# A Transformer block on one Trainium2 core: the order of gates, outputs, norms and index work in the retention stage

## The chip, the cores and the metric

The kernel runs on one core of a Trainium2 chip. A core has a matrix engine (TensorE, PE in the profile; PEld is its weight load), three engines for elementwise work (VectorE or DVE, ScalarE or ACT, GpSimd or POOL), and SyncE (SP), which here only issues DMAs. Each engine works through its own queue in order and waits on semaphores for the others. The time is the device time of one execution in microseconds (us), lower is better; three executions of the kernel before give 1562.02, 1562.23 and 1563.64, a median of 1562.23.

## The reference

One hybrid block over 512 tokens of width 1024 and 16 meta tokens ahead of them (528 in all): a gated feed-forward layer, a mixer, a second gated feed-forward layer, with norms between. The mixer projects the normed input `u` with one wide matrix and feeds two branches:

```python
proj = u @ w_in   # rq, rk, rv, rg, aq, ak, av, iq, ik, iw, g_ret, g_att
yr = retention(rope(rq), rope(rk) * 256**-0.5, rv)     # 4 heads, keys 256, values 512 wide
yr = (silu(rg) * yr) @ w_ret_out                       # yr is normed per head first
ya = dsa_attention(rope(aq), rope(ak), av, rope(iq), rope(ik), iw, 128) @ w_att_out
merged = sigmoid(g_ret) * yr + sigmoid(g_att) * ya
```

Retention is a product of queries and keys, weighted by a decay matrix per head, times the values, and each head's result is divided by its root mean square over its 512 values. Attention has 8 heads of 128. For each query an index score is worked out first: `sum over 8 index heads of iw * relu(iq . ik)`; the 128 best keys by that score (and the meta tokens) are the only ones that the attention of that query sees.

## The kernel before

All products are taken in three parts: both operands are split into an upper and a lower half (`hi`, `lo`), and `mm3` (line 145) issues hi x hi, lo x hi and hi x lo. So each weight tile needs an upper half on ACT (line 284), a lower half on DVE (line 285) and then 24 matmuls, 8 depth blocks of three.

The kernel goes in stages: the first feed-forward layer, projections of values and index and of head 0's queries and keys, the retention stage (about 555 to 924 us), attention (924 to 1116 us), the output projections, the second feed-forward layer. The change lies in the retention stage and the first 20 us of attention.

The retention stage is a list of steps, one for each weight tile, that `steps_through` (line 289) runs: at step i it issues the DMA of tile i+4, the upper half of tile i+2, then the step's matmuls, then the lower half of tile i+2, and then whatever stands "behind" the step. Work may also be put between the depth blocks of a step (`between`: at block k, do this). The order on PE, ACT and DVE is the order in which the program is written (`tc.manual_schedule`); SP and POOL are planned. PSUM has a small pool of four banks (`sm_tile`) for tiles of 512 columns and a second pool of two (`mm_tile`).

Per head h of the four:

- `gates_of(h)` (line 1536): four steps that make psrg; `silu` puts each through ACT into an `sg` buffer, of which there are two. Behind them for h > 0: `values_in(h)`, which splits the values into `vo` hi and lo, and `weigh(h, c)` for c = 0, 1, 2.
- `decayed(h)` (line 1421): the products of keys and queries (psst, 30 matmuls in five tiles), each multiplied on DVE by the decay table `u` (line 1439) and split.
- `weigh(h, c)` (line 1460): 13 matmuls into pspv, multiplied on DVE by the gate (line 1467) into a `to` tile, squares added to `ossum` on ACT and DVE.
- `norm_start(h)` and the generator `rstd_steps`: column sums of `ossum` by four small matmuls (line 218), power on POOL (line 227), a diagonal on DVE (line 232), split, and a product with ones that spreads the result over all rows (psn, line 242), copied to `rn`.
- `normed_parts(h)`: four products `to` times `rn` (line 1487), each split into `vo` hi and lo again, in the place of the values.
- `outputs(h)` (line 1634): four steps of 2 x 12 matmuls into psro, which read those `vo` parts; the result is added to the accumulators `accr`. In the first step, SP fetches the next head's values and decay table; behind the last stands `decayed(h+1)`.
- `queries_keys(h)` (line 1590): four steps for the next head's queries and keys, rotated on DVE in pieces (`rope_pieces`).

The order is: gates of head 0; then for h = 1 to 3: queries_keys(h), outputs(h-1), gates_of(h); then two gate tiles (psgate), the first key and query tile of attention (psak, psaq), outputs(3), one more gate tile. Head h-1's last `weigh` and its norm stand behind the steps of queries_keys(h), `normed_parts(h-1)` behind the last of them, right ahead of outputs(h-1).

The index scores are made beside this. `bring_index` (line 1338), at the first gate of head 0, has the inputs brought: `ixs` (index queries, two copies), the tables `cos` and `sin`, the decay table `u`, head 0's values (`vraw`, four DMAs), and the index keys. `index_queries(0..3)` rotate and split the queries (three DVE operations of 1536 columns, one split). `index_steps` (line 1238) makes the scores in twelve "pairs": six matmuls into two pssc tiles, two relus on ACT, two multiply-and-adds on DVE (line 1257). Before, all pairs lie in queries_keys(1), three in each of its four steps. `select_steps` (line 1262) then draws 48 "picks" on DVE: find the 8 largest of a row (line 1269), mark them (line 1270); 16 each for score tiles of 512, 384 and 256 columns. After each 16, one operation makes a bias tile. Picks stand one to three at a time behind later steps; attention needs the bias tiles in turn.

After the steps, attention's first key and query are rotated by `rope_swap` (line 1225): two half copies on ACT, a product with cos on DVE, one with sin on POOL, a sum on DVE. Then come two gate tiles and the first scores (psS).

## Time and profile before

The profiled execution took 1563.07 us, 0.84 above the median of the three; its span is 1561.3 us at a mean granted TensorE clock of 0.99.

| what | before |
|---|---|
| median of three executions | 1562.23 us |
| profiled execution, span | 1563.07, 1561.3 us |
| PE busy | 1527.3 us, 98% |
| DVE busy | 1092.4 us, 70% |
| ACT busy | 728.7 us, 47% |
| POOL busy | 105.7 us, 7% |
| the stretch 555.5 to 936.3: PE, DVE, ACT busy | 357.34, 263.24, 136.81 of 380.8 us |

How to read it: a line such as `L1435 MATMUL psst<-rqk` is line 1435 of the kernel before, engine operation, the tile written and the tiles read. Matmuls are pipelined: a matmul of 512 columns shows 0.39 us, and the next one begins 0.23 us after it. A wait row names who waited for what and for how long. In a row of a stretch of time the numbers after the length are busy times per engine, then the granted clock (1.00 is full speed), then the share of the DMA engines in use and GB/s. "idle before" in a group of instructions is the time that the engine stood still ahead of them, with the last thing that it waited for.

### The profile page before, as it was taken

The numbers are of one execution on the slowest core, as the hardware profiler recorded it, in microseconds if no ns is written. First come the engines' busy times: TensorE is split into PE (matmuls) and PEld (weight loads), VectorE is DVE, ScalarE is ACT, GpSimd is POOL, SyncE is SP. The second block draws the span as 40 slices with busy tenths as digits, with TensorE's granted clock in tenths as the row PEclk, the third lists the DMA queues.
The fourth block names the chain that finished last, engine by engine and source line by source line (L and its number), as shares of the span: only waits on it lengthen the run. The fifth ranks groups of instructions, "written<-read, shape, count | busy, mean of one in ns | idle before, by whom it ended". The sixth has DMA issues, their size and how long they took to land.

```text
span 1561.3 us, 23921 instructions
## 1 busy us (share of the span) xinstructions
PE 1527.3 (98%) x9779; PEld 1374.8 (88%) x9779; DVE 1092.4 (70%) x1670; ACT 728.7 (47%) x1138; POOL 105.7 (7%) x135
## 2 busy tenths in 40 slices
PE   9999999999999979899999999999999999999997
PEld 8999999999888867687888878999888889899996
DVE  4997585776877756667777687666455788576685
ACT  6655362554354434333323337666435446254453
POOL 1000000002110020000000031111002000000000
PEclk9999999999999989899999999999999999999999
DMA  4233233237364271222322233233443223323232
GB/s 164 70 121 101 90 102 115 82 122 237 129 223 148 82 221 42 101 99 76 118 69 82 96 106 100 75 97 89 137 154 114 81 81 109 108 83 135 82 112 91
DMA packets 150701, 173.48 MB, mean 111 GB/s; under 512 B 4928, under 2 KB 122200, under 8 KB 149952
## 3 DMA queue, kind: packets, MB, share of 16 engines
q1 hardware_dynamic: 141952, 151.58, 29.9%
q0 software_dynamic: 3808, 11.38, 2.0%
q10 hardware_dynamic: 4832, 9.00, 1.7%
q8 instruction: 76, 1.25, 0.3%
q14 instruction: 33, 0.27, 0.1%
HBM read 155.94 MB, written 16.01 MB: 110 GB/s over the span
## 4 chain that ended last, share of the span: by engine, by line
PE 85%; issue 7%; DVE 4%; ACT 2%; DMA 1%; POOL 1%; POOLq 0%; ACTq 0%; DVEq 0%
PE psqX L157 13%; PE psd L157 8%; PE psd L2035 7%; PE psqY L157 7%; PE psro L157 4%; PE psvX L1120 4%; PE psrg L157 4%; PE psqZ L157 3%; PE psu L157 3%; PE psga L157 3%; PE psmo L157 3%; PE psat L157 3%; PE psak L157 3%; PE psaq L157 2%; PE psg L157 2%
## 5 line engine op out<-in xcount | busy, mean ns | idle before, releaser
L285 DVE TENSOR_TENSOR wlo<-raw,whi 128x1024 fp32r<-128x1024 f32 (+2 forms) x184 | 197.4, 1076 | 65.7 <-ACT whi L284 65.6
L284 ACT ACTIVATE whi<-raw 128x1024 fp32r<-128x1024 f32 (+2 forms) x184 | 170.0, 925 | 135.3 <-PE psd L157 41.2
L157 PE MATMUL psqX<-tl,whi 128*128 128x264 f32 (+1 forms) x432 | 122.3, 283 | 0.0
L157 PE MATMUL psqX<-th,wlo 128*128 128x264 f32 (+1 forms) x432 | 122.2, 283 | 0.0
L157 PE MATMUL psqX<-th,whi 128*128 128x264 f32 (+1 forms) x432 | 122.2, 283 | 0.0
L118 DVE TENSOR_TENSOR wlo<-raw,whi 128x1024 fp32r<-128x1024 f32 (+1 forms) x60 | 72.3, 1205 | 56.7 <-ACT whi L117 55.7
L284 ACT ACTIVATE whi<-wsum 128x1024 fp32r<-128x1024 f32 x72 | 76.4, 1061 | 70.7 <-PE psd L2035 22.0
L117 ACT ACTIVATE whi<-raw 128x1024 fp32r<-128x1024 f32 (+1 forms) x60 | 62.6, 1045 | 93.9 <-PE psat L157 26.6
L285 DVE TENSOR_TENSOR wlo<-wsum,whi 128x1024 fp32r<-128x1024 f32 x72 | 87.9, 1222 | 12.5 <-ACT whi L284 12.5
L157 PE MATMUL psro<-vo,whi 128*128 128x512 f32 x256 | 86.0, 415 | 10.2 <-ACT vo L284 9.5
L157 PEld LDWEIGHTS psqX<-th,whi 128*128 128x128 f32 x432 | 82.1, 190 | 0.0
L157 PEld LDWEIGHTS psqX<-tl,whi 128*128 128x128 f32 x432 | 82.0, 190 | 0.0
L157 PEld LDWEIGHTS psqX<-th,wlo 128*128 128x128 f32 x432 | 82.0, 190 | 0.0
L157 PEld LDWEIGHTS psro<-vo,whi 128*128 128x128 f32 x256 | 50.6, 198 | 25.6 <-ACT vo L284 10.2
L157 PE MATMUL psd<-hl,whi 128*128 128x264 f32 x352 | 71.2, 284 | 0.0
L157 PE MATMUL psd<-hh,wlo 128*128 128x264 f32 x352 | 70.9, 283 | 0.0
L157 PE MATMUL psd<-hh,whi 128*128 128x264 f32 x352 | 70.6, 282 | 0.0
L2035 PE MATMUL psd<-whi,hh 128*128 128x512 f32 x176 | 68.5, 389 | 0.0
L2035 PE MATMUL psd<-wlo,hh 128*128 128x512 f32 x176 | 68.5, 389 | 0.0
L2035 PE MATMUL psd<-whi,hl 128*128 128x512 f32 x176 | 68.5, 389 | 0.0
L157 PEld LDWEIGHTS psd<-hh,wlo 128*128 128x128 f32 x352 | 54.4, 188 | 0.0
L157 PEld LDWEIGHTS psd<-hh,whi 128*128 128x128 f32 x352 | 54.3, 188 | 0.0
(440 smaller groups left out, 4529.8 us busy)
## 6 DMA issues: line engine op xcount, KB each, us to landing
raw<-in_ffn_w_up_dram SPq DMA_DIRECT2D x22, 1024.0 KB, 5.0
raw<-in_ffn_w_gate_dram SPq DMA_DIRECT2D x21, 1024.0 KB, 5.0
raw<-in_w_in_dram SPq DMA_DIRECT2D x19, 1024.0 KB, 4.9
raw<-in_w_in_dram SPq DMA_DIRECT2D x31, 512.0 KB, 3.5
raw<-in_ffn_w_down_dram SPq DMA_DIRECT2D x24, 512.0 KB, 3.4
w<-in_w_in_dram SPq DMA_DIRECT2D x24, 512.0 KB, 6.8
raw<-in_ffn_w_down_dram SPq DMA_DIRECT2D x12, 768.0 KB, 4.3
raw<-in_w_ret_out_dram SPq DMA_DIRECT2D x8, 1024.0 KB, 4.7
```

The lines of the kernel that those rows point to most:

```text
L117: nc.scalar.activation(hi, src, AF.Copy)
L118: eng.tensor_tensor(lo, src, hi.bitcast(F32), ALU.subtract)
L157: nc.tensor.matmul(o, a[:, k, :], b[:, sl], start=first and k == 0 and i == 0, stop=last and k == nk - 1 and i == 2, skip_group_check=onto)
L284: nc.scalar.activation(hi, src, AF.Copy)
L285: return lambda: nc.vector.tensor_tensor(lo, src, hi.bitcast(F32), ALU.subtract)
L1120: nc.tensor.matmul(d[bank_][t], a, b[:, k, :], start=not onto and j + k + m == 0, stop=j + k == 3 and m == 2, skip_group_check=onto)
L2035: nc.tensor.matmul(ps, a[:, bs], m[:, j, :], start=first and i == 0, stop=last and i == 2)
```

## The change

- Each head's gates stand ahead of the outputs of the head before: the order is queries_keys(h), gates_of(h), outputs(h-1); of the last head only three gates do, the fourth stands behind. For this there are four `sg` buffers.
- `weigh(p, 0..3)` of head p = h-1 stand one behind each step of queries_keys(h). `values_in(h+1)` moves behind outputs(h).
- The norm is cut in pieces: sums at block 6 inside the first gate, the diagonal behind it, the spreading product at block 4 inside the second gate, and the normed parts two and two behind the second and the third.
- `bring_index`: `u` and the four `vraw` DMAs go first on SP. `decayed(0)` stands ahead of all index queries, and the index keys and the rest of the index queries follow later.
- The pairs: two in the last step of queries_keys(1), then 2, 2, 3 and 3 in the four gates of head 1.
- The picks are drawn at other places and fewer beside each step; those left follow behind the last steps.
- At the start of attention the fifth and sixth gate tile and the first rotation stand in program order too, and the rotation's product with sin goes to DVE.

The diff, cut; where the removed lines are long they are left out, since the kernel before shows them.

```diff
--- before.py
+++ after.py
...
@@ -1231,7 +1229,7 @@
             nc.scalar.activation(bv[hi], ps[lo], AF.Copy)
             nc.scalar.activation(bv[lo], ps[hi], AF.Copy)
         nc.vector.tensor_tensor(av, ps, cos, ALU.mult)
-        nc.gpsimd.tensor_tensor(b[:, :n], b[:, :n], sin, ALU.mult)
+        eng.tensor_tensor(b[:, :n], b[:, :n], sin, ALU.mult)
         nc.vector.tensor_tensor(a[:, :n], a[:, :n], b[:, :n], ALU.add)
         return a[:, :n]
@@ -1336,16 +1334,16 @@
         heads = [dict(t=[], sg=[], o=[]) for _ in range(RH)]
         def bring_index():
+            new_decay(0)
+            heads[0]["raw"] = [rt.tile([P, S], F32, tag="to", name="vraw", bufs=4) for _ in range(4)]
+            for c in range(4):
+                nc.sync.dma_start(heads[0]["raw"][c], vst[0, :, c].rearrange("p b d -> p (b d)"))
             nc.sync.dma_start(ia[:, :, :NL], fq[:, :, :NL])
             for r in range(4):
                 o = r ^ 1
                 nc.gpsimd.dma_start(ib[32 * r : 32 * r + 32, :, :NL], fq[32 * o : 32 * o + 32, :, :NL])
             for i, t in enumerate((cosi, sini)):
                 nc.sync.dma_start(t, rope[0, i, :, REAL])
-            new_decay(0)
-            heads[0]["raw"] = [rt.tile([P, S], F32, tag="to", name="vraw", bufs=4) for _ in range(4)]
-            for c in range(4):
-                nc.sync.dma_start(heads[0]["raw"][c], vst[0, :, c].rearrange("p b d -> p (b d)"))
             nc.gpsimd.dma_start(ka[:64, :S], fs[:64, 0, :])
             for r in range(2):
                 nc.gpsimd.dma_start(kb_[32 * r : 32 * r + 32, :S], fs[32 * (1 - r) : 32 * (2 - r), 0, :])
...
@@ -1469,27 +1473,52 @@
             d["t"].append(t)
         def silu(h, ps):
...
+            sg = rt.tile([P, S], F32, tag="sg", name="sg", bufs=4)
             nc.scalar.activation(sg, ps, AF.Silu)
             heads[h]["sg"].append(sg)
...
+        def norm_sums(h):
             d = heads[h]
+            col = sm_tile("psn")
+            for b in range(4):
+                nc.tensor.matmul(col[:, b : b + 1], d["ssum"][:, b * P : (b + 1) * P], ones, start=True, stop=True)
+            ms = rt.tile([P, 5], F32, tag="ms", name="ms", bufs=2)
+            nc.vector.tensor_scalar(ms[:, :4], col[:, :4], 1.0 / DV, EPS, ALU.mult, ALU.add)
+            r = d["rcol"] = rt.tile([P, 5], F32, tag="rcol", name="rcol", bufs=2)
+            nc.gpsimd.tensor_tensor(r[:, :4], ms[:, :4], mhalf[:, :4], ALU.pow)
+        def norm_diag(h):
+            d = heads[h]
+            diag = tmp()[:, :S]
+            d["diag"] = hi, lo = [tmp()[:, :S].bitcast(F32R) for _ in range(2)]
+            TT(diag.rearrange("p (b c) -> p b c", b=4), ident.unsqueeze(1).to_broadcast([P, 4, P]),
+               d["rcol"][:, :4].unsqueeze(2).to_broadcast([P, 4, P]), ALU.mult)
+            return in_two(diag, hi, lo)
+        def norm_all(h):
+            d = heads[h]
+            ps = sm_tile("psn")
+            for i, part in enumerate(d["diag"]):
+                nc.tensor.matmul(ps, ones_r, part, start=i == 0, stop=i == 1)
             d["rn"] = rt.tile([P, S], F32, tag="rn", name="rn")
...
+            nc.scalar.activation(d["rn"], ps, AF.Copy)
+        def normed_parts(h, c):
+            d = heads[h]
+            TT(d["t"][c], d["t"][c], d["rn"], ALU.mult)
+            o = tuple(p[:, c, :] for p in vr["parts"])
+            d["o"].append(o)
+            return in_two(d["t"][c], *o)
+        def two_normed_parts(h, c):
+            lows = [normed_parts(h, c + i) for i in range(2)]
+            for low in lows:
                 low()
...
         raws = {}
@@ -1535,48 +1564,56 @@
         def gates_of(h):
+            p = h - 1
             def behind_0(ps):
                 silu(h, ps)
+                if h:
+                    low = norm_diag(p)
+                    if h > 1:
+                        pick(1)
+                    low()
+            def behind_1(ps):
+                silu(h, ps)
                 if h == 0:
+                    decayed(0)
                     index_queries(0)
+                else:
+                    two_normed_parts(p, 0)
+            def behind_2(ps):
+                silu(h, ps)
+                if h == 0:
                     index_queries(1)
+                    index_queries(2)
                 else:
...
+                    two_normed_parts(p, 2)
+            def behind_3(ps):
+                silu(h, ps)
                 if h == 0:
...
                     index_queries(3)
+                    values_in(0)
+                    picks["pairs"] = index_steps()
+                    picks["steps"] = select_steps()
+                elif h == 1:
+                    for _ in picks["pairs"]:
+                        pass
                 else:
...
+                    if h == RH - 1:
+                        weigh(h, 0)
+                    pick(3)
+            sums, spread = (6, lambda: norm_sums(p)), (4, lambda: norm_all(p))
+            inside = [()] * 4
+            if h == 1:
+                inside = [((1, pair), (4, pair), sums), ((1, pair), spread, (6, pair)), ((1, pair), (4, pair), (6, pair)),
+                          ((1, pair), (3, pair), (6, pair))]
+            elif h:
+                some_picks = (3, lambda: pick(1))
+                inside = [(sums,), (spread,), (some_picks,), (some_picks,)]
+            runs = [proj("psrg", REAL, i, b) for i, b in zip(inside, (behind_0, behind_1, behind_2, behind_3))]
             if h == 0:
                 run0 = runs[0]
@@ -1590,45 +1627,36 @@
         def queries_keys(h):
             pss, p = {}, h - 1
...
+            ropes = heads[h]["ropes"] = {}
             def q0(ps):
                 pss["qa"] = ps
...
+                if h == 1:
+                    index_keys(0)
+                    index_keys(1)
+                weigh(p, 0)
+                if h == 1:
+                    index_keys(2)
             def q1(ps):
                 pss["qb"] = ps
...
+                ropes["q"] = rope_pieces(pss["qa"], ps, cos[:, REAL], sin[:, REAL], S, ret_q)
+                some(ropes["q"], 5)
+                weigh(p, 1)
             def k0(ps):
                 pss["ka"] = ps
...
+                some(ropes["q"], 1)
+                weigh(p, 2)
+                some(ropes["q"], 1)
             def k1(ps):
...
+                ropes["k"] = rope_pieces(pss["ka"], ps, cos, sin, T, ret_k)
+                weigh(p, 3)
+            inside = ((3, pair), (6, pair)) if h == 1 else ()
+            return (steps_of(tiles(("rq", h), w_in, OFF_RQ + h * DK, 2), [proj("psrq", REAL, (), q0), proj("psrq", REAL, (), q1)])
+                    + steps_of(tiles(("rk", h), w_in, OFF_RK + h * DK, 2), [proj("psrk", None, (), k0), proj("psrk", None, inside, k1)]))
         def outputs(h, beside):
@@ -1649,16 +1677,13 @@
                             heads[h + 1]["raw"] = raw
                         else:
                             vr["raw"] = raw
-                    pss = []
                     for j in range(2):
                         ps = sm_tile("psro")
                         mm3([(ps, slice(0, S))], [t[:, :, j * P : (j + 1) * P] for t in w],
                             lambda k: heads[h]["o"][k], DV // P)
-                        pss.append(ps)
                         if j == 0:
                             lower()
                             beside(i)
-                    for j, ps in enumerate(pss):
                         a = acc_r[2 * i + j]
                         if h == 0:
                             nc.scalar.activation(a, ps, AF.Copy)
@@ -1666,6 +1691,7 @@
                             TT(a, ps, a, ALU.add)
                     if i == 3 and h + 1 < RH:
                         decayed(h + 1)
+                        values_in(h + 1)
                 return run
             return steps_of(tiles(("ro", h), w_ro[h * DV : (h + 1) * DV, :], 0, 4, DV // P, 2 * P), [step(i) for i in range(4)])
@@ -1673,45 +1699,49 @@
         def beside_outputs(h):
             def beside(i):
                 if i < 3:
-                    heads[h + 1]["ropes"]["k"][i]()
-                else:
-                    pick(1)
+                    some(heads[h + 1]["ropes"]["k"], (3, 3, 1)[i])
+                pick(2 if h == 0 and i == 2 else 1)
             return beside
         last_gates, first_kq = [], []
         def keep_gate(ps):
-            t = rt.tile([P, S], F32, tag="sg", name="gate", bufs=2)
+            t = rt.tile([P, S], F32, tag="sg", name="gate", bufs=4)
             nc.scalar.activation(t, ps, AF.Sigmoid)
             last_gates.append(t)
+        p = RH - 1
         def last_0(ps):
-            pick(3)
-            weigh(RH - 1, 3)
             keep_gate(ps)
+            weigh(p, 1)
+            weigh(p, 2)
         def last_1(ps):
-            pick(3)
             keep_gate(ps)
-            norm_start(RH - 1)
+            weigh(p, 3)
+            pick(2)
         def last_2(ps):
             first_kq.append(ps)
-            next(heads[RH - 1]["norm"])
-            pick(2)
-            next(heads[RH - 1]["norm"])
+            low = norm_diag(p)
+            pick(1)
+            low()
         def last_3(ps):
             first_kq.append(ps)
-            normed_parts(RH - 1)
+            two_normed_parts(p, 0)
+            two_normed_parts(p, 2)
         more = gates_of(0)
         for h in range(1, RH):
-            more += queries_keys(h) + outputs(h - 1, beside_outputs(h - 1)) + gates_of(h)
+            gates = gates_of(h)
+            n = 4 - (h == p)
+            more += queries_keys(h) + gates[:n] + outputs(h - 1, beside_outputs(h - 1)) + gates[n:]
         more += steps_of(tiles("gr", w_in, OFF_GR + 2 * P, 2), [proj("psgate", REAL, (), last_0), proj("psgate", REAL, (), last_1)])
-        more += steps_of(tiles("ak", w_in, OFF_AK, 1), [proj("psak", None, (), last_2)])
-        more += steps_of(tiles("aq", w_in, OFF_AQ, 1), [proj("psaq", REAL, (), last_3)])
-        more += outputs(RH - 1, lambda i: pick(2))
+        more += steps_of(tiles("ak", w_in, OFF_AK, 1), [proj("psak", None, ((4, lambda: norm_sums(p)),), last_2)])
+        more += steps_of(tiles("aq", w_in, OFF_AQ, 1), [proj("psaq", REAL, ((3, lambda: norm_all(p)),), last_3)])
+        more += outputs(p, lambda i: pick(2))
         more += steps_of(tiles("gr4", w_in, OFF_GR + 4 * P, 1), [proj("psgate", REAL, (), first_kq.append)])
         steps += more
         with tc.manual_schedule(engines=BUSY):
...
@@ -1871,11 +1901,16 @@
                     nc.sync.dma_start(gd[KD + ga.at - 1], t)
             place_tails(4)
-            k, q = rope_k(first_k), rope_q(first_q)
-            t = at.tile([P, S], F32, tag="gate", name="gate", bufs=2)
-            nc.scalar.activation(t, first_gate, AF.Sigmoid)
-            gate_acc(4, t)
-            wide_gate()
+            with tc.manual_schedule(engines=BUSY):
+                w = gr.next()
+                k, q = rope_k(first_k, nc.vector), rope_q(first_q, nc.vector)
+                t, t5 = (at.tile([P, S], F32, tag="gate", name="gate", bufs=2) for _ in range(2))
+                nc.scalar.activation(t, first_gate, AF.Sigmoid)
+                gate_acc(4, t)
+                ps = mm_tile("psgate")[:, :S]
+                mm3([(ps, REAL)], w, xs, KD)
+                nc.scalar.activation(t5, ps, AF.Sigmoid)
+                gate_acc(5, t5)
             for h in range(AH):
                 more = h + 1 < AH
                 scores(q, k)
```

129 lines of the change are left out of this document (33 added, 96 removed).

## The prediction

> **What bounds the kernel now.** I read the page first, then TensorE's waits in the stretch that the change touches, then that stretch cut into pieces with the granted clock, then the queues behind each wait.
>
> ```profile
> span 1561.3 us, 23921 instructions
> PE 1527.3 (98%) x9779; PEld 1374.8 (88%) x9779; DVE 1092.4 (70%) x1670; ACT 728.7 (47%) x1138; POOL 105.7 (7%) x135
> ```
>
> TensorE is busy for 98% of the span, and the change takes no matrix product away. So it can only win where PE stands still or runs at a lower clock. Where PE waits between 555 and 937 us:
>
> ```profile
> PE psro L157 <- ACT vo L284: 9.5, 3, 3.7
> PE psst L1435 <- DVE tmp L1439: 9.0, 1, 9.0
> PE psn L242 <- ACT tmp L117: 3.1, 1, 3.1
> PE psS L1834 <- ACT aq L117: 1.0, 1, 1.0
> PE psro L157 <- DVE vo L285: 0.7, 3, 0.2
> ```
>
> Columns: what waited and for what, us in total, times, longest. It is 23.3 us in nine waits. The same stretch in pieces (start:end, length, busy time of the engines in turn, then the granted clock, the DMA share and GB/s):
>
> ```profile
> 555.50:578.70 23.20, 14.25 (x67) 11.88 (x65) 8.74 (x8) 5.83 (x7) 8.11 (x22) 0.91 0.97 284
> 578.70:599.60 20.90, 20.84 (x100) 17.93 (x100) 15.28 (x25) 11.40 (x20) 0.00 (x0) 0.86 0.25 85
> 630.00:637.00 7.00, 4.75 (x22) 3.86 (x23) 6.21 (x10) 1.26 (x2) 0.00 (x0) 0.76 0.00 0
> 646.50:675.80 29.30, 29.25 (x127) 23.85 (x127) 17.20 (x25) 12.57 (x19) 0.00 (x0) 0.89 0.31 103
> 733.50:762.00 28.50, 28.23 (x127) 22.74 (x127) 22.46 (x33) 8.34 (x11) 0.00 (x0) 0.94 0.32 104
> 818.90:847.30 28.40, 28.17 (x126) 22.72 (x127) 22.14 (x33) 8.31 (x11) 0.00 (x0) 0.94 0.32 105
> 924.20:936.30 12.10, 11.07 (x50) 8.84 (x48) 10.67 (x14) 8.24 (x12) 7.90 (x12) 1.00 0.40 111
> ```
>
> Behind each wait of three us or more the granted clock is under 1.00, though PE is busy there nearly all the time. What that costs is length times what the clock lacks: 20.9 x 0.14 = 2.9 us after the psst wait, 7.0 x 0.24 = 1.7 around the psn wait, 29.3 x 0.11 = 3.2, 28.5 x 0.06 = 1.7 and 28.4 x 0.06 = 1.7 after the three entries into psro. Together 11.2 us. The Trainium skill ("TensorE: Matmul & The Clock Gate", section "Part 1: The HAM clock gate") says that TensorE falls to half clock after an idle window of about 3.4 us and comes back after as long a busy one. The trace agrees in kind, but waits of 3.12 and 3.27 us brought it too, so a wait need not be a whole window long here.
>
> So waits and clock hold 23.3 + 11.2 = 34.5 us. More than that the change cannot win.
>
> The 9.0 us wait, seen on PE, in SP's queue and on DVE:
>
> ```profile
> 566.39 3.36 PE L1435 MATMUL psst<-rqk 128*128 128x512 f32 x18
> 578.76 1.79 PE L1435 MATMUL psst<-rqk 128*128 128x256 f32 x12 [9.01 <-DVE tmp L1439]
> ```
> ```profile
> 556.64 0.62 SPq L1339 DMA_DIRECT2D ixs<-fq  x1
> 565.60 0.34 SPq L1344 DMA_DIRECT2D cos<-in_rope_dram  x1
> 565.99 0.42 SPq L1344 DMA_DIRECT2D sin<-in_rope_dram  x1
> 566.46 0.43 SPq L1385 DMA_DIRECT2D u<-in_decay_dram  x1
> 566.93 1.85 SPq L1348 DMA_DIRECT2D vraw<-vst  x4
> ```
> ```profile
> 571.87 1.76 DVE L1363 TENSOR_TENSOR ixs<-ixs,cos 128x1536 f32<-128x1536 f32 x1 [13.21 <-DMA cos<-in_rope_dram]
> 573.55 1.75 DVE L1363 TENSOR_TENSOR ixs<-ixs,sin 128x1536 f32<-128x1536 f32 x1
> 575.22 1.22 DVE L285 TENSOR_TENSOR wlo<-raw,whi 128x1024 fp32r<-128x1024 f32 x1
> 576.35 1.75 DVE L1365 TENSOR_TENSOR ixs<-ixs 128x1536 f32<-128x1536 f32 x1
> 578.02 1.17 DVE L1439 TENSOR_TENSOR tmp<-psst,u 128x512 f32<-128x512 f32 x2
> ```
>
> DVE works in program order. It stood at the first index product until the rotation table landed (cos was issued at 565.60, SP being held for 9 us behind ixs), then did three index operations, and only then the decay product that frees the PSUM banks of psst.
>
> **The change part by part.** Prices of the operations on DVE and ACT:
>
> ```profile
> L285 DVE TENSOR_TENSOR wlo<-raw,whi 128x1024 fp32r<-128x1024 f32 x47 | 57.5, 1224 | 36.1 <-ACT whi L284 36.1
> L285 DVE TENSOR_TENSOR vo<-to,vo 128x512 fp32r<-128x512 f32 x16 | 11.0, 689 | 0.8
> L1487 DVE TENSOR_TENSOR to<-to,rn 128x512 f32<-128x512 f32 x16 | 10.6, 685 | 0.0
> L1269 DVE MAX8 top<-score 128x8 f32<-128x256 f32 x16 | 6.8, 424 | 0.3
> L1270 DVE MATCH_REPLACE8 score<-top,score 128x256 f32<-128x256 f32 x16 | 6.5, 409 | 0.0
> L1257 DVE SCALAR_TENSOR_TENSOR score<-tmp,wt,score 128x512 f32<-128x512 f32 x7 | 5.3, 752 | 3.6 <-ACT tmp L1255 3.2
> ```
> ```profile
> L227 POOL TENSOR_TENSOR rcol<-ms,mhalf 128x4 f32<-128x4 f32 x4 | 6.7, 1676 | 106.0 <-DVE ms L225 106.0
> ```
> ```profile
> L284 ACT ACTIVATE vo<-to 128x512 fp32r<-128x512 f32 x16 | 10.0, 632 | 15.4 <-DVE to L1487 15.4
> L1255 ACT ACTIVATE tmp<-pssc 128x512 f32<-128x512 f32 x8 | 4.4, 596 | 3.7 <-PE pssc L1252 3.7
> L1366 ACT ACTIVATE iqh<-ixs 128x1536 fp32r<-128x1536 f32 x1 | 1.5, 1486 | 15.4 <-DVE ixs L1365 15.4
> ```
>
> *Decay product ahead of the index queries.* On SP u and the four vraw now stand ahead of ixs, cos and sin. u takes SP's free place at about 557, and must have landed by the first psst at 566. It is half the size of ixs, and ixs together with what stood before it had landed by 571.87, so I take it as there in time. The wait of 9.0 goes, and with it the 2.9 us of clock: 11.9 us. What is late next is the index work. vraw now stands where cos was held until 565.60, and ixs, cos, sin come after. The DMA share of 0.97 up to 578.7 and 0.25 after it says that all these inputs are in by about 577; the last in line land last, so I put cos at 576.7 instead of 571.8. From there DVE needs four index operations of 1.75 (7.0), two weight splits of 1.22 (2.4), a stay of about 1.5 for ACT's iqh between the third and fourth, and one low half of the values (0.69): 576.7 + 11.6 gives 588.3, or 589.3 where a split's upper half is behind iqh on ACT. PE gets there after 5 us of psst, two gates and q0 of 5.5 us each: 566.4 + 5 + 16.5 = 587.9. The first weigh, now in q0, waits 0.4 to 1.4, and the values' halves may add some: I take 1.8, with 0 (inputs no later than before) and 4 (cos at 579) as ends.
>
> *The norm in pieces, pairs spread.* The psn wait (3.1) goes because between the sums and the broadcast product lie now the end of one gate and half of the next, and the 1.7 us of clock go with it: 4.8. What comes instead: the broadcast stands at k=4 of the second gate, 2.7 us after its start; the diagonal needs a product, an upper and a lower half (0.69 + 0.63 + 0.69 = 2.0 us) after POOL's power (1.68, begun after the sums at k=6, some 4.5 us into the first gate), which ends about 0.8 us into that gate, so it is about 0.5 us late: three heads, 1.5. In the last head it stands at k=3 of aq with picks ahead of it: 1.0. Together 2.5, ends 1 and 4.
>
> Ten of the pairs go into head 1's gates. A pair needs two of the four banks of the small pool; a gate has one, so a second pair waits for the first one's two relus (0.6 each at 512 wide). In the second and third gate these stand on ACT behind silu and two upper halves of vo (0.63), which themselves follow DVE's product (0.69 each). One relu behind such a chain is 1.6 to 2.0 us late, once in each of two or three gates: I take 3.8. The ends are 2 (one gate alone) and 7 (each of three gates, with a weight split of 1.22 ahead).
>
> *Gates ahead of the outputs.* The normed values that psro reads are now made beside the third gate or earlier, so all three entry waits go: 9.5 + 0.7, and 3.2 + 1.7 + 1.7 of clock, 16.8 us. The cover is one gate of 5.5 us against two products, two upper and two lower halves (4 us). Before outputs(2) it is only three gates, and the last two parts follow that gate's silu on ACT; PE has 1.4 us of the first two parts to do, a stay of 0.3 or so that I leave in the 2.5 above. The two more gate buffers, values_in at the end of outputs and the moved decay table of the next head cost nothing on PE: DVE is busy 22.46 of 28.5 us there and loses the normed products' tail.
>
> *The end.* Here the change costs. Fewer picks are drawn beside the gates, so twelve of width 256 stand after the last psro, woven into DVE's queue with the preparation of attention.
>
> ```profile
> 936.25 0.63 PE L1834 MATMUL psS<-ak,aq 128*128 128x400 f32 x2 [1.03 <-ACT aq L117]
> ```
> ```profile
> 930.29 1.78 DVE L1235 TENSOR_TENSOR tmp<-tmp 128x528 f32<-128x528 f32 x1 [1.23 <-POOL tmp L1234]
> 936.59 0.68 DVE L118 TENSOR_TENSOR aq<-tmp,aq 128x512 fp32r<-128x512 f32 x1
> ```
>
> From the last psro at 924.2 to the low half of aq DVE now takes 13.1 us (to 937.27), PE's two gates 11.0. Afterwards DVE has seven picks (0.424 + 0.409, about 0.86 with the small load: 6.0), two value splits (2.4), a weight split (1.2), six rotation products (0.69, issued each 0.6: 3.7) and two low halves (1.3): 14.6, and some 0.3 of starts. So the third score product waits 1.7 us longer, and the transposes of the second bias, whose picks come later still, another 1.7: 3.4 us. The ends are 1 (the rotation gains more) and 6 (all twelve picks, 4.3 us more, ahead of what PE waits for, 2.6 of them felt). The rotation's sine product leaves POOL for DVE: DVE gets two operations more, and the sum of 1.78 us becomes short (products 512 wide take 0.69). The Trainium skill ("SBUF — State Buffer", section on the two separate sides) says that a DVE operation with two SBUF inputs and a GpSimd operation that reads SBUF lock each other out of a shared port; the 1.78 us row beside POOL's product agrees, and by it the move gives about 1.1 us back, which the count above holds already.
>
> **Sum.** Gone: 11.9 + 4.8 + 16.8 = 33.5. Come: 1.8 + 2.5 + 3.8 + 3.4 = 11.5. Net 22.0 us off the profiled execution's 1563.07, 1541.1. That execution is 0.84 above the median of 1562.23, so on the median's basis 1540.2; I say 1540. With the ends of the new waits (1 + 2 + 0 + 1 = 4, and 4 + 4 + 7 + 6 = 21) it is 1533 to 1550.
>
> **The rivals.**
>
> *All the new waits are covered: 1532.* Then only some 3 us of the new waits stay. For it: DVE, busy 22 of 28 us in the outputs, has slack in them. Against it: the queues are in program order, and aq has a count of operations that no slack shortens.
>
> *The end is worse: 1549.* If all twelve picks precede aq, DVE needs 18.9 us against PE's 11.0, a wait of nearly 8, and like the waits of three us above it brings a spell of lower clock (1.7 to 3.2): 6 to 9 us more than the 3.4. For it: the piece 924.2 to 936.3 has DVE busy 10.67 of 12.10 already. Against it: attention's operations stand between the picks in the order, and not behind.
>
> *It doesn't do what it says: 1551.* The entry waits come back in smaller form, 2 to 3 us each with their clock, because ACT's upper halves of vo are behind the pairs' relus and silu. About 11 of the 16.8 us stay. For it: ACT has one queue. Against it: a whole gate of 5.5 us lies between, except in outputs(2).
>
> *Slower: the index inputs come late, 1567.* Place: DVE's queue at the first index product. Behind it stand the weight splits of q0 and the values, so PE stops as soon as those are due. SP stood for 9 us once in this stretch, and cos landed 6.3 us after its issue; with two more such holds behind vraw and that transfer after them, cos lands at 576.7 + 18 + 6.3 = 601. PE's wait is then 24.3 us longer than my 1.8, and with 3 us of clock that is 27.3 - 22 = 5.3 slower. It decides from cos at about 596: 22 us of gain less 3 of clock make 19 us behind 576.7. Against it: the DMA share falls to 0.25 after 578.7, so the same bytes are in by then in the kernel before.
>
> **How the numbers follow.** Forecast 0.62; all covered 0.12; the end worse 0.11; entry waits remain 0.07; late index inputs or another wait of that size 0.06; the last 0.02 is a gain eaten up by chance. A measurement of this kernel can tell about 0.2%, 3.1 us, from no change. Faster 0.62 + 0.12 + 0.11 + 0.07 = 0.92, same 0.02, slower 0.06. The range runs from the covered case, 1531, to beyond the case in which entry waits remain, 1553.
>
> **What would show it.** In the profile after: no psst wait and a clock of 1.00 around 575 to 585; no psro wait of over a us, and 1.00 in the three output stages; no psn wait of 3 us; instead small waits at pspv in q0, at pssc or psrg in head 1's gates, and at psS 2 to 3 us with MAX8 rows after the last psro. The prediction is wrong if a wait of over 4 us stands at psS or in head 1, if cos lands after 580, or if PE's clock drops at a place where it was 1.00.

## The result

The changed kernel takes 1543.46 us (median of 1541.07, 1542.76, 1544.16 and 1546.00) against 1562.47 of the kernel before, measured beside it: a ratio of 0.9877, with an interval of 0.986 to 0.9895. That is 19 us less; forecast were 22, a time of 1540 and a range of 1531 to 1553. A second set of four gave 1543.56. The profiled execution took 1541.07, where the sum of the prediction gave 1541.1; it is also the shortest of its four, which is told below.

The page of the kernel after, to be held against the two lines of before:

```profile
span 1539.3 us, 23919 instructions
PE 1518.3 (99%) x9779; PEld 1368.7 (89%) x9779; DVE 1092.5 (71%) x1672; ACT 727.2 (47%) x1138; POOL 105.7 (7%) x133
```

TensorE does the same 9779 matmuls in 9.0 us less busy time, since more of them ran at the full clock. The rest of the 22.0 us of span is 13.0 us of standing still that is gone. Where PE still waits between 550 and 925 us (who for what, us, times, longest):

```profile
PE pspv L1460 <- ACT vo L282: 2.9, 1, 2.9
PE psS L1864 <- ACT aq L117: 2.0, 1, 2.0
PE psS L1864 <- DVE aq L118: 1.9, 1, 1.9
PE pssc L1250 <- ACT tmp L1253: 1.7, 2, 1.1
PE psn L1506 <- DVE tmp L283: 1.1, 2, 0.6
PE psro L157 <- DVE vo L283: 0.5, 2, 0.2
```

Each big wait of before has gone (psst 9.0, psro on ACT 9.5, psn on ACT 3.1), and each wait named in the prediction has come. In pieces of time, the granted clock being the third number from the end:

```profile
555.50:581.60 26.10, 26.10 (x129) 22.01 (x128) 11.56 (x16) 10.03 (x15) 8.25 (x22) 1.00 0.98 297
653.13:679.20 26.07, 26.07 (x126) 21.82 (x125) 20.41 (x33) 11.20 (x17) 0.00 (x0) 1.00 0.38 122
734.20:760.30 26.10, 26.10 (x128) 21.86 (x126) 25.60 (x45) 6.88 (x9) 0.00 (x0) 1.00 0.37 122
809.80:836.50 26.70, 26.47 (x127) 21.75 (x126) 22.96 (x40) 8.05 (x11) 0.00 (x0) 1.00 0.30 98
902.00:920.00 18.00, 14.16 (x61) 11.58 (x60) 17.93 (x42) 9.57 (x13) 2.95 (x2) 0.91 0.40 125
```

The first row held a 9 us hole before, and PE is now busy in it from end to end. The three output stages (653, 734, 810) stood at 0.89, 0.94 and 0.94 and now have the full clock. One place is new: 902 to 920, the start of attention, at 0.91, which is 18 x 0.09 = 1.6 us. In the kernel before this place stood at 1.00, so here one of the signs of being wrong that the prediction named has come: a clock that drops where it was 1.00.

The new wait at pspv, as SP's queue and DVE show it:

```profile
556.73 0.55 SPq L1383 DMA_DIRECT2D u<-in_decay_dram  x1
557.38 2.07 SPq L1340 DMA_DIRECT2D vraw<-vst  x4
560.34 0.61 SPq L1341 DMA_DIRECT2D ixs<-fq  x1
566.00 0.34 SPq L1346 DMA_DIRECT2D cos<-in_rope_dram  x1
```
```profile
577.41 1.76 DVE L1361 TENSOR_TENSOR ixs<-ixs,cos 128x1536 f32<-128x1536 f32 x1 [4.34 <-DMA cos<-in_rope_dram]
...
587.50 1.75 DVE L1366 TENSOR_TENSOR iql<-ixs,iqh 128x1536 fp32r<-128x1536 f32 x1
590.00 2.50 DVE L283 TENSOR_TENSOR vo<-vraw,vo 128x512 fp32r<-128x512 f32 x4 [0.74 <-ACT vo L282]
```
```profile
589.34 2.19 ACT L282 ACTIVATE vo<-vraw 128x512 fp32r<-128x512 f32 x4 [2.52 <-issue]
```

cos is in at 577.3, 11.3 us after its issue (forecast 576.7), and the values' halves begin only at 589.3 on ACT, right behind the last index operation. In the code the two tiles of `vo` bear the tags of the two tiles of `ixs`, so the values go into the memory that the index queries leave.

The end, PE and then DVE:

```profile
912.46 2.79 PE L1864 MATMUL psS<-ak,aq 128*128 128x400 f32 x13 [1.89 <-DVE aq L118]
```
```profile
910.94 1.47 DVE L118 TENSOR_TENSOR aq<-tmp,aq 128x512 fp32r<-128x512 f32 x1
912.33 0.42 DVE L1267 MAX8 top<-score 128x8 f32<-128x256 f32 x1
912.67 1.96 DVE L118 TENSOR_TENSOR wlo<-raw,whi 128x1024 fp32r<-128x1024 f32 x1
```

Picks stand between the operations that aq waits for, as was forecast.

### The profile page after: what moved, and what is told of

Its sections match the earlier page's. It is cut to its first block, busy times and chain, and to the rows that moved or that the text cites. A ratio compares the mean times of both kernels' runs of the same rounds, so it can differ in the third digit from the quotient of the medians.

```text
span 1539.3 us, 23919 instructions
## 1 busy us (share of the span) xinstructions
PE 1518.3 (99%) x9779; PEld 1368.7 (89%) x9779; DVE 1092.5 (71%) x1672; ACT 727.2 (47%) x1138; POOL 105.7 (7%) x133
## 4 chain that ended last, share of the span: by engine, by line
PE 85%; issue 10%; DVE 2%; ACT 1%; POOL 1%; DMA 1%; SPq 0%; ACTq 0%; POOLq 0%; DVEq 0%
PE psqX L157 14%; PE psd L157 8%; PE psd L2070 7%; PE psqY L157 7%; PE psvX L1118 4%; PE psro L157 4%; PE psqZ L157 3%; PE psak L157 3%; PE psu L157 3%; PE psga L157 3%; PE psmo L157 3%; PE psat L157 3%; PE psaq L157 3%; PE psg L157 2%; PE psgate L157 2%
## 5 line engine op out<-in xcount | busy, mean ns | idle before, releaser
L157 PE MATMUL psro<-vo,whi 128*128 128x512 f32 x256 | 80.3, 394 | 0.5 <-DVE vo L283 0.5
L157 PEld LDWEIGHTS psro<-vo,whi 128*128 128x128 f32 x256 | 48.1, 188 | 11.9 <-DVE vo L283 1.1
```

The costliest lines, as they stand in the source:

```text
L157: nc.tensor.matmul(o, a[:, k, :], b[:, sl], start=first and k == 0 and i == 0, stop=last and k == nk - 1 and i == 2, skip_group_check=onto)
```

## The experiments

Each kernel was run beside the kernel before, whose medians lay between 1562.65 and 1562.86 us. "After" is 1543.5.

**One part alone, on the kernel before: before_decay.**

```diff
 def bring_index():
+    new_decay(0); four vraw DMAs
     nc.sync.dma_start(ia ...)
...
-    new_decay(0); four vraw DMAs
 # behind the second gate
-    index_queries(2); silu(0, ps); decayed(0); index_queries(3)
+    silu(0, ps); decayed(0); index_queries(0..3)
```

> The kernel before with one part of the change: u and vraw first in SP's queue, and the decay product ahead of all four index operations behind the second gate. If the parts of the sum can be had one by one, the psst wait of 9.0 us and 2.9 us of clock go, less 1.8 of a new wait: 1552 us. My theory after seeing the profile of the change is another: the index chain then ends at about 586 whatever stands ahead of it, the values' halves come after it, and the first weigh of this kernel stands behind the third gate, where PE arrives at about 576. So the wait moves from psst to pspv, 10 to 12 us with its clock, and the time stays at 1561 to 1565 us.

Measured: 1564.88 us (ratio 1.0015, interval 1.0006 to 1.0025), 2 us slower than before. Its waits:

```profile
PE pspv L1456 <- ACT vo L284: 10.4, 1, 10.4
PE psro L157 <- ACT vo L284: 9.5, 3, 3.6
```

The wait of 9.0 at psst became one of 10.4 at pspv. The decay product ahead of the index work is worth nothing by itself. The change also moves the first weigh from behind the third gate to behind q0, two steps of 5.5 us later, and so gives the index chain time. That this move is what makes the part pay is argued from the order of the steps; no run moves the first weigh alone. The prediction put it into its arithmetic (the arrival at 587.9) but did not say that the part rests on it.

**The same part undone in the changed kernel: dec_undo, and half of it: sp_old.**

```diff
 # both: bring_index
-    new_decay(0); four vraw DMAs; ixs; ...; cos; sin
+    ixs; ...; cos; sin; new_decay(0); four vraw DMAs
 # dec_undo only, behind the second gate
-    decayed(0); index_queries(0)
+    index_queries(0..2); decayed(0)
```

> The changed kernel with the whole of one part undone: SP's old order, and on DVE three index operations ahead of the decay product again. Theory: the wait at psst comes back as in the kernel before, 9 to 11 us with 2.9 of clock, and the wait of 2.9 at the first pspv goes: 8 to 11 us above the changed kernel, 1551 to 1554 us. By the run in which this part was done alone it was worth nothing; if it is worth nothing here too, 1543.

> The changed kernel with SP's old order in bring_index: ixs, cos, sin, then u and vraw. DVE's order stays that of the change. My theory: both are needed. u lands at about 574 as in the kernel before, psst waits for it for 4 to 5 us and brings 1.7 to 2.9 us of lower clock, while the first weigh's wait of 2.9 stays within 1 us of that or shrinks: 1546 to 1550 us, 3 to 6 above the changed kernel. Rival: only DVE's order counts, then the time is that of the changed kernel, 1543.

Measured: 1547.83 us and 1546.21 us. One row of each, dec_undo first:

```profile
PE psst L1439 <- DVE tmp L1443: 7.5, 1, 7.5
```
```profile
PE psst L1439 <- DVE tmp L1443: 5.1, 1, 5.1
```

sp_old came out as expected: without the new DMA order psst waits for the decay table, as DVE shows:

```profile
575.21 1.17 DVE L1443 TENSOR_TENSOR tmp<-psst,u 128x512 f32<-128x512 f32 x2 [10.87 <-DMA u<-in_decay_dram]
```

dec_undo is 4.3 above after, about half of what was expected. By the spans of the profiled executions it is more, 1546.3 against 1539.3 and 1540.0, some 6.5; those two of after are the shortest of their fours. The wait that came back is 7.5 and not 9 us, and the pspv wait of 2.9 left in exchange. So the part is worth 4 to 7 us where the prediction netted 10.1 (11.9 less 1.8).

**vraw behind the index inputs: vraw_last.**

```diff
 def bring_index():
     new_decay(0)
-    four vraw DMAs
     ixs; ...; cos; sin
+    four vraw DMAs
```

> The changed kernel with SP's order u, ixs, cos, sin, vraw: the four vraw DMAs behind the index inputs instead of ahead. Theory: the 2.9 us wait at the first pspv comes from cos and ixs landing at 577; with 1 MB less ahead of them they land 2.5 to 3.5 us sooner and the wait falls to 0 to 0.7: 1540 to 1541 us. Rival: the DMA engines are full in that stretch and SP is held by the value stores anyway, so cos lands at 576 to 577 as now and the time stays at 1543.

Measured: 1537.77 us, four runs within 0.8 us. The pspv wait is gone, and DVE starts the index chain 4.2 us sooner than in after:

```profile
573.24 1.76 DVE L1361 TENSOR_TENSOR ixs<-ixs,cos 128x1536 f32<-128x1536 f32 x1
```

The gain is 5.7 us, twice the wait that was removed, and more than the theory expected. The next run bears on why.

**After once more: after_again.**

> The changed kernel once more, unchanged, beside the three others. Four runs of it lay between 1541.1 and 1546.0, while vraw_last's four lay within 0.8 us. If the spread comes from the clock behind the pspv wait of 2.9 us, which falls in some executions and not in others, this run again spreads over 3 us or more, and the longer ones show a lower granted clock.

Measured: 1541.78, 1543.30, 1543.82, 1545.40, with mean granted clocks of 0.997, 0.995, 0.996 and 0.994; by spans, 1540.0, 1541.5, 1541.0 and 1543.5, the order is that of the clock. The spread is there again: 0.003 of 1540 us is 4.6 us of clock, enough for the 3.6 us between the shortest and the longest. vraw_last has no such spread, and of the waits between 550 and 945 us all it lacks is the 2.9 us at pspv. So that wait costs its 2.9 us and, probably, in most executions a spell of lower clock as well; the two profiled executions would be among those without. This is not shown: no profile holds such a spell behind pspv in a kernel of this order. The spell at psS can differ too (behind waits of some 1.9 and 1.9 us it is 3.4 us long in after and 6.8 in dec_undo and sp_old), and best_dve below spreads over 3.4 us without any wait at pspv.

**The clock alone: before_fill.** Extra matmuls on PE while it stands before psro; nothing else is changed.

```diff
 # outputs(h), first step, ahead of the first psro product
+    for k in range((15, 13, 13)[h]):
+        nc.tensor.matmul(ps, w[0][:, 0, :P], xs(k % KD)[0][:, REAL], start=True, stop=True)
```

> The kernel before with 15, 13 and 13 extra matmuls of 512 columns ahead of the first matmul of outputs(0), (1), (2); they write a PSUM tile that the next matmul overwrites, and take 3.4, 2.9 and 2.9 us where PE stood still for 3.7, 3.3 and 3.3. No work is taken away and psro starts no earlier. If the lower clock behind those waits comes from PE's standing still, the granted clock in the three output stages is 1.00 and 6.6 us go: 1556 us. If the clock falls there for another reason, or if the fillers delay psro, it stays at 1562 to 1563.

Measured: 1561.29 us, ratio 0.9991 (0.9982 to 1.0001). The clock did what was expected, the time did not. Stretches and waits:

```profile
630.00:637.00 7.00, 4.77 (x20) 4.00 (x20) 6.21 (x10) 1.26 (x2) 0.00 (x0) 0.60 0.00 0
640.00:676.00 36.00, 35.06 (x174) 28.36 (x175) 23.36 (x37) 14.72 (x25) 0.00 (x0) 1.00 0.27 88
728.00:762.00 34.00, 32.97 (x159) 26.56 (x158) 26.32 (x40) 11.35 (x17) 0.00 (x0) 1.00 0.29 93
815.00:848.00 33.00, 32.42 (x152) 26.02 (x152) 26.51 (x43) 10.68 (x17) 0.00 (x0) 1.00 0.30 96
```
```profile
PE psro L157 <- DVE vo L285: 2.1, 9, 0.2
PE psro L157 <- ACT vo L284: 0.6, 2, 0.3
```

The three output stages are at 1.00: PE's standing still is what lowers the clock. But psro's first products now wait nine times for DVE's halves of vo (2.1 us) instead of three times (0.7): the pace at which vo is made holds them, at the lower clock and at the full one. From the end of psrk to the first matmul of psst the three stages are 1.45, 0.63 and 0.62 us shorter in the profiled execution, 2.7 together, and the slow spell at 632 happened to be longer (0.60 against 0.76, 1.1 us). The third entry's wait of before was 2.6 us on ACT and not 3.3, so its fillers end 0.2 us late. So less than half of the 6.6 us of clock were to be had by themselves; in after all of it goes, where the parts are there before psro begins.

**The normed parts right ahead of psro again: v_norm_late.** This and the next three start from vraw_last, which spreads less.

```diff
 # gates_of(1) and gates_of(2)
 behind_1:  silu
-           two_normed_parts(p, 0)
 behind_2:  silu
-           two_normed_parts(p, 2)
 behind_3:  silu; the last pairs (h == 1)
+           two_normed_parts(p, 0); two_normed_parts(p, 2)
```

> The changed kernel with vraw behind the index inputs (vraw_last, 1537.8 us), and with the normed parts of heads 0 and 1 made only behind the fourth gate, right ahead of outputs(0) and outputs(1), instead of behind the second and third gate. My theory: a whole gate between these parts and psro is what took the entry waits away. Without it psro waits 3 to 3.7 us for ACT's upper half of vo at two of three entries, and the first outputs step runs at the pace of DVE's halves: 5 to 6.5 us for each, 1548 to 1551 us. Rival: the parts are quick enough beside psro's first products now that weigh and the norm come earlier, 1 us each: 1540.

Measured: 1545.73 us, 8.0 above vraw_last, for two entries. Waits, and the clock behind the first:

```profile
PE psro L157 <- ACT vo L282: 4.0, 3, 2.4
...
PE psro L157 <- DVE vo L283: 0.9, 4, 0.2
```
```profile
649.50:653.50 4.00, 3.75 (x9) 2.51 (x10) 3.81 (x7) 2.64 (x5) 0.00 (x0) 0.57 0.80 262
```

So a gate between the parts and their use is worth 4 us an entry, net of the 1.7 us at pssc, which are gone here. That is less than the 5 to 6.5 expected: the first waits at the two entries are 2.4 and 1.2 us, where before they were 3.7 and 3.3. Why they are shorter was not tried. The rival (1 us each) falls.

**The left-over picks drawn earlier: v_picks.**

```diff
 # heads 2 and 3
 q0: weigh(p, 0)
+    pick(2)
 q1: weigh(p, 1)
+    pick(1)
 k0: weigh(p, 2)
+    pick(1)
 behind_3:
-    pick(3)
+    pick(4)
 # last_0: pick(1) more, last_1: pick(3) for pick(2)
```

> vraw_last (1537.8 us) with the twelve left-over picks drawn earlier: two, one and one behind q0, q1 and k0 of heads 2 and 3, one more behind two gates and two more in the last steps, so none stands in DVE's queue at the start of attention. My theory: they are what makes psS wait 3.9 us and what lowers the clock behind it (some 2 us), and DVE has room beside queries_keys; the psS waits fall to 0 to 1 us and the time to 1532 to 1534 us. Rival: the picks come back as waits where they now stand (behind weigh, ahead of the norm), each 512 wide one 1.4 us: 1537 to 1540 us.

Measured: 1534.06 us, 3.7 below vraw_last, within the expected 1532 to 1534 but for a hair. The psS waits fell from 3.9 to 2.2 us, not to 0 to 1, the 0.9 us at psao is gone, and the clock stays at 1.00 in the profiled execution:

```profile
906.62 0.63 PE L1871 MATMUL psS<-ak,aq 128*128 128x400 f32 x2 [1.49 <-ACT aq L117]
907.96 1.92 PE L1871 MATMUL psS<-ak,aq 128*128 128x400 f32 x13 [0.71 <-DVE aq L118]
```
```profile
904.00:913.00 9.00, 6.80 (x35) 5.34 (x35) 7.76 (x17) 7.46 (x13) 3.04 (x2) 1.00 0.60 189
```

**The product with sin back on POOL: v_pool.**

```diff
-k, q = rope_k(first_k, nc.vector), rope_q(first_q, nc.vector)
+k, q = rope_k(first_k), rope_q(first_q)
```

> vraw_last (1537.8 us) with the product with sin at the start of attention back on POOL. One theory: on DVE it costs two operations of 0.69 us ahead of aq's low half, so without them DVE's chain is 1.2 us shorter and the time 1536.6 us. The other: beside POOL's product DVE's operations with two SBUF inputs take 1.2 to 1.8 us instead of 0.7 to 1.2, and DVE waits for POOL's 2.3 and 1.3 us; there are more such operations beside it now, and the time is 1538.5 to 1541 us. I hold the second.

Measured: 1538.22 us, 0.45 above vraw_last with ranges that overlap (1537.19 to 1538.42, 1537.66 to 1538.46): no difference. One of the two psS waits is gone, the other stays:

```profile
907.59 3.34 PE L1864 MATMUL psS<-ak,aq 128*128 128x400 f32 x13 [1.89 <-DVE aq L118]
```

In exchange there is a new one behind it, 0.8 us at psPT for DVE's pj.

POOL's two products took 1.33 and 1.31 us and DVE's sums behind them 0.70, not 1.78: neither of my theories, the second above all, is borne out. The second sum began at 903.65, when POOL's product, begun at 902.31, had just ended, so this run has the two side by side nowhere and doesn't tell whether they hold each other up. Moving the product to DVE gained nothing in the time, and the prediction was wrong to count 1.1 us for it.

**The pairs spread: v_space.**

```diff
-((1, pair), (4, pair), (6, pair)), ((1, pair), (3, pair), (6, pair))
+((2, pair), (5, pair), (7, pair)), ((2, pair), (5, pair), (7, pair))
```

> vraw_last (1537.8 us) with the pairs of head 1's third and fourth gate at blocks 2, 5 and 7 instead of 1, 4, 6 and 1, 3, 6. Theory: the second pair waits for the first one's relus, which stand on ACT behind two upper halves of vo and one of a weight; given 0.7 and 1.4 us more, the two pssc waits (1.7 us in all) fall to 0.5 or less and the time by 1.2 to 1.7: 1536 to 1536.6 us. Rival: the last pairs then come too late and psro waits for a bank as long: 1537.8 us.

Measured: 1538.51 us against 1537.77: no gain in the time. Yet the pssc waits fell as expected, from 1.7 to 0.3:

```profile
PE pssc L1250 <- ACT tmp L1253: 0.3, 1, 0.3
```

The profiles tell where the 1.4 us went. The stretch at the start of attention, first in v_space, then in vraw_last:

```profile
907.00:916.00 9.00, 7.77 (x28) 6.80 (x29) 8.93 (x21) 3.69 (x5) 2.30 (x2) 0.62 0.78 234
```
```profile
907.00:916.00 9.00, 7.11 (x31) 6.09 (x30) 8.93 (x23) 4.65 (x7) 2.95 (x2) 0.81 0.66 207
```

The same two waits at psS (1.9 and 1.9 us) are followed by a lower clock in both, for 6.8 us in v_space and 3.4 in vraw_last: 9 x (0.81 - 0.62) = 1.7 us. What sets the length is told in the last section; whether the stall that is gone 260 us earlier has a part in it, one profile of each can't tell.

**All together: best_dve and best_pool**, that is vraw_last with v_picks and v_space, and the same with the product on POOL.

> vraw behind the index inputs, the left-over picks drawn earlier, and the pairs of two gates spread (blocks 2, 5, 7). With the picks gone, no wait of 3 us is left whose spell of low clock could eat the pairs' gain, so it should now show: 1534.1 less 1.2 to 1.4, 1532.7 us. If spreading the pairs truly gains nothing: 1534.

> The same with the product with sin back on POOL: DVE then has two operations of 0.69 us less ahead of aq's low half, for which PE still waits 2.2 us: 1531.5 us. If POOL's product and DVE's operations hold each other up: 1533 to 1535.

Measured: 1534.67 us (1532.89 to 1536.30) and 1533.07 us (1532.06 to 1533.67). best_pool has the lowest median of all, 0.9809 of before (0.9794 to 0.9824) and 10.4 us under after, 1.0 under v_picks with ranges that just touch. Spreading the pairs again does not show in the time. best_dve has the waits of v_picks to a hundredth, and yet not its clock:

```profile
906.21 0.63 PE L1871 MATMUL psS<-ak,aq 128*128 128x400 f32 x2 [1.49 <-ACT aq L117]
907.55 2.74 PE L1871 MATMUL psS<-ak,aq 128*128 128x400 f32 x13 [0.71 <-DVE aq L118]
```
```profile
904.00:913.00 9.00, 6.80 (x29) 5.42 (x28) 7.75 (x21) 7.46 (x13) 3.03 (x2) 0.81 0.55 168
```

0.81 against 1.00 over 9 us is 1.7 us, more than the pairs could give. best_pool lacks the second wait, and its one wait of 1.5 us on ACT is followed by 3.4 us of lower clock all the same.

## Why the prediction was right

*Which waits hold the time.* Right. Waits and clock of 34.5 us were all that could be won in the prediction's window; just past it lies one more wait of before. After the change the waits of this stretch are 10.1 us, the clock 1.6, and one more wait, in the first product with the values of attention, 0.9. First before, then after:

```profile
PE psS L1834 <- DVE aq L118: 0.4, 1, 0.4
```
```profile
PE psao L1461 <- issue: 0.9, 1, 0.9
```

Together 12.6; 34.5 + 0.4 - 12.6 = 22.3, against 22.0 measured between the two profiled executions.

*Decay product first.* The mechanism is right: u was there in time, cos landed 0.6 us later than said, and the wait moved to the first weigh. That wait is 2.9 us where I took 1.8 (ends 0 to 4). The step that was missing: ACT's upper halves of the values can't begin before the last index operation is done with that memory. The terms around it (0.7 for ACT's first half, and the stay for iqh, 2.5 us where I took 1.5) were set too short, and PE arrived 0.7 us sooner than I said. That wait of 2.9, with what goes with it, is 5.7 us by vraw_last where I had 1.8; it is the main reason why the median lies 3.5 us above the forecast.

*Norm in pieces.* 1.1 us at psn against 2.5 taken (ends 1 and 4): nearly 0.6 in each of two heads, none in the first one's norm and none in aq.

*Pairs.* 1.7 us at pssc against 3.8 (ends 2 and 7): just under the lower end. The cause is the one named, relus behind vo's halves on ACT: the wait shrinks when the pairs come later (v_space), and is gone when the vo halves are moved out of those gates (v_norm_late).

*Gates ahead of the outputs.* Right: 0.5 us of the 10.2 remain, and all of the clock came back. v_norm_late shows the gate between to be the cause, and before_fill that the 6.6 us of clock and the waits were not independent: with the waits filled, 2.7 us of it went in the three stages.

*The end.* 3.9 us at psS instead of 1.0 and 0.4, and 0.9 at psao, are 3.4 us of waits, just what I took (ends 1 and 6), though the 0.9 was said for the transposes and came behind them. To this come 1.6 us of clock. The step that failed is the one that held the clock out of it: the two psS waits are 2.0 and 1.9 us, and I had counted a lower clock only for a wait of nearly 8. Moving the picks away is worth 3.7 us (v_picks).

*From the profile to the median.* Less the 1.4 us at psS that were there before, what came is 12.6 - 1.4 = 11.2 us where 11.5 were forecast. That is luck in part: pspv is 1.1 over, the end 1.6 and psro 0.5, and the norm 1.4 and the pairs 2.1 under. I also carried the offset of the kernel before (0.84) over to the kernel after, whose profiled execution is 2.4 us under its median; so the forecast of the profiled execution fits to 0.1 us and that of the median to 3.5.

*The rivals.* "All covered" (1532) did not come, though vraw_last with the picks moved comes to about 2 us of it, so the waits can be covered. "The end is worse" has its sign right, by 1.6 us of clock where it said 6 to 9; its condition, all twelve picks ahead of aq, did not come: seven stand there, as the prediction's own count had it. The entries did not come back, and the late index inputs were 0.6 us late and not 24.

## What to carry to other kernels

In a chain with one critical resource, a wait taken away is worth what the next wait behind it leaves: before_decay turned 9.0 us at one place into 10.4 at another, while in the changed kernel, where the consumer comes later, the same part is worth 4 to 7. When DMAs are reordered, put first what starts the longest chain and last what is used at the chain's end; here four transfers moved behind three others were worth 5.7 us. Price a wait on TensorE with its spell of lower clock, as a chance and not as a constant, and compare medians rather than two profiled executions.

## What was unexpected of the hardware

The lower clock does not follow from the length of a wait alone. The waits of 1.49 and 0.71 us at psS left the clock at 1.00 in v_picks and brought 0.81 over 9 us in best_dve; a pair of 1.9 us waits brought a spell twice as long in v_space as in vraw_last; and the 2.9 us at pspv left 1.00 in the profiled executions of after.

What decides it can be read from the traces. In the fourteen profiles the granted clock is either 1.00 or 0.50, and any two of its changes in an execution lie a whole multiple of 3.413 us apart, so the spells are 3.4, 6.8, 10.2 or 13.7 us long. Here are rows cut along this grid, one for each of its pieces (called windows here), two of best_dve and two of v_picks; the length less PE's busy time is how long PE stood still:

```profile
904.91:908.33 3.42, 1.41 (x7) 1.07 (x8) 2.17 (x4) 3.40 (x6) 1.47 (x1) 1.00 0.66 177
908.33:911.74 3.41, 3.41 (x14) 3.08 (x13) 3.41 (x13) 3.38 (x7) 1.56 (x2) 0.50 0.53 150
```
```profile
903.60:907.02 3.42, 1.93 (x9) 1.24 (x7) 2.73 (x4) 2.00 (x3) 0.00 (x0) 1.00 0.84 299
907.02:910.43 3.41, 2.70 (x19) 2.33 (x18) 2.87 (x11) 3.39 (x5) 3.04 (x2) 1.00 0.83 238
```

In best_dve 2.0 us of the waits lie in one window, and the next window is at 0.50. In v_picks the same waits are spread over two windows, 1.5 and 0.7 us, and the clock stays at 1.00. So it does in after at pspv, whose 2.9 us are spread as 1.7 and 1.1. Over all windows between 550 and 950 us, full clock was lost behind every one with 1.77 us or more of standing still and behind none with 1.75 or less, but for one of 1.56 us in best_pool. A spell went on where its own window held 0.44 us or more (v_space: 2.8 us, then 0.75) and ended where it held 0.23 or less. The grid lies elsewhere in each execution, 0.6 us apart in the two of after, so for a wait of 2.9 us the spell is a chance: an estimate from these figures is that it comes in eight or nine of ten positions of the grid.

The Trainium skill ("TensorE: Matmul & The Clock Gate", section "Part 1: The HAM clock gate") says that the window in which idleness is counted runs freely, and that the penalty varies from run to run for that reason. That agrees with these runs. But its idle window of about 3.4 us need not be idle throughout: 1.6 to 2.1 us in one window of the grid were enough here.

The stretched DVE operations at the start of attention did not come from the product with sin. In after, where that product is on DVE, aq's low half took 1.47 us (0.68 before) and the weight split 1.96 (elsewhere 1.22). What ran on POOL at that time in these kernels is the product of the accumulators with their gates:

```profile
910.60 2.95 POOL L1320 TENSOR_TENSOR accr<-accr,gate 128x512 f32<-128x512 f32 x2 [10.79 <-ACT gate L1908]
```

The rest of the trace of after says the same. All 15 subtractions of 512 or 1024 columns that began on DVE while a product ran on POOL were stretched, to 1.37 to 1.82 us at 512 columns and to 1.57 to 2.01 at 1024. Of the other 413 one was more than 5% over the usual 0.69 or 1.22. Eight of these 413 were under way when a product on POOL began, and seven of the eight times it is POOL's product that took longer, 1.85 to 2.13 us in place of 1.3. So the one that begins second is held up. What keeping these products of POOL away from aq's low half would be worth was not tried.
